# A transformer layer on one core: where 26 gate rows are loaded, where a bias correction is turned, and when eight sub-norms run

## The chip, the cores and the metric

The kernel runs on one core of a Trainium2 chip. Its time is the device time of one execution in microseconds (us); the kernel before took 2425.93 us, the median of three runs (2421.64 to 2428.02). A core has five engines with an instruction queue each, and each works through its queue in order: PE (matrix products; PEld is its loading of the stationary operand), DVE (vector), ACT (scalar and copies), POOL, and SP, which here only issues DMA transfers. POOL issues transfers too, in a queue of its own.

## The reference, cut to what matters

One layer of a diffusion transformer over 512 latent tokens and 256 context tokens, width 2048, everything in float32. Six modulation vectors come from a product of a conditioning vector with a 2048 x 12288 matrix; context tokens have their own conditioning.

```python
mod_x = (silu(c) @ w_ada + b_ada)                  # 6 x 2048, cut into sh1, s1, g1, sh2, s2, g2
h  = rmsnorm(x, norm1_w) * (1 + s1) + sh1          # the same for the context with c_ctx
p  = h @ w_in                                      # q, k, v of 8 differential heads; latent q, latent kv, a shared rotary key
o_da  = rmsnorm(softmax(q1 k1') v - lam * softmax(q2 k2') v, subln_w) * 0.8      # 8 heads
o_mla = softmax(([q_nope, q_rope] . [k_nope, k_rope]) / sqrt(192)) v             # 8 latent heads
x  = x + g1 * (concat(o_da, o_mla) @ w_o)
h2 = rmsnorm(x, norm2_w) * (1 + s2) + sh2
x  = x + g2 * ((silu(conv3(h2 @ w_up_gate)) * (h2 @ w_up_u)) @ w_down)
out = rmsnorm(x, final_w)
```

## The kernel before, in words

Tokens lie along the free dimension, features on the 128 partitions. Every float32 product is made of three products of a coarser type: an operand is split into a high part (a cast on ACT) and a rest (a subtraction on DVE), and `mm3` (L107, L108, L109) multiplies high by high, high by rest and rest by high. A block of weights is 128 x 1024; it is loaded by SP into one of the `wr` buffers, cast to `wh` on ACT and its rest `wl` taken on DVE. The third product of a block needs its rest.

Each of the 96 rows of 128 modulation values is a product that DVE makes alone: `gemv` loads a 1 MB piece of the matrix into one of two `ada` buffers and multiplies it with the conditioning vector in one instruction (L174). 64 of these rows are made late, one at a time between other work (`next_gemv`): those of s2 first, then of g1, sh2 and g2. A row's load into a buffer waits for the product that read the buffer last.

The input projection is a list of steps whose order is written out by hand on all engines (a "manual schedule"). Step i runs a block on PE, casts block i+2 on ACT, runs its first task, takes the rest of block i+2 on DVE and issues the load of block i+4 on SP, and then runs its other tasks (`step`). The first 16 row blocks were multiplied before their shift was known, so for the first features a correction is made: `bias_products` puts the products of the shifts into two PSUM banks, `bias_rows` copies them to SBUF, `bias_turn` turns them into columns with six small products (L729), and `bias_out` copies the columns to `beta` (L733). The two banks are the ones that the next feature block needs. Steps 2 to 9 make the values of the first four heads (`value_block(0, ...)`, 12 pairs of column half and token tile each), step 10 is the first half of feature 1, step 11 its second half, and so on; `feature_keys` rotates a feature and writes it out as keys; `lay(t)` splits and writes a tile of values.

Behind the projection the order within each engine comes from a scheduler that looks at the code's order, the engines and the buffers. The differential heads write their outputs to memory. The latent heads come in pairs: `latent_pair` projects queries, keys and values of a pair, and is called while the pair before is running; each head makes its scores (which read the shared rotary keys `krh` and `krlz`, loaded once, L1014 and L1017), its softmax, one `sub_norm` of a differential head (L1023 to L1028: a load, a square on ACT, one product on PE, a root on ACT and DVE, six DVE instructions in all), and `weighted_values`, which transposes the weights into a bank `pt`, or with its last argument set into two more banks `f` besides.

The output projection has four groups of eight blocks (`w_o[g, kb]`). Each block has 24 products on PE. At the end of a group four tiles of `x` are loaded into three buffers `xr`, DVE adds the scaled result (L1116) and POOL writes it out. Before most blocks stands a gate row of `next_gemv`, loaded by POOL. At the head of this stage the code of before reads

```python
            if g or kb > 2:
                next_gemv(wo, 1, gp)
            wh, wl = wblock(w_o[g, kb])
```

Then come the gated MLP (two thirds of the time) and the final norm, in a manual schedule again.

Of the kernel before, what the change touches and what calls it, by code (L numbers as in the profile page):

```python
# [9 lines left out]
F32 = mybir.dt.float32  # L10
# [42 lines left out]
def layer_kernel(ctx: ExitStack, tc: tile.TileContext, small, rope, c_row, cc_row, x_t, ctx_t, ada, ada_k,  # L53
# [484 lines left out]
    def gemvs(count):  # L538
        return lambda: next_gemv(sp_, count, gp)
# [127 lines left out]
                if 1 in g and co is not None:  # L667
                    mm3(co, w, hc[kt], kt == 0, kt == KT - 1)

    def value_block(half, vo, n_, last):  # L670
        wh, wl = hl_w.pop(len(steps))
        order = [(j, t) for t in last for j in range(2)] if n_ == 7 else [(j, t) for j in range(2) for t in range(NKEY)]
        for j, t in order:
            kt = KB[half][n_] * 2 + j
            w = (wh[:, j * 512:(j + 1) * 512], wl[:, j * 512:(j + 1) * 512])
            src, o = (hx[kt], t * P) if t < 4 else (hc[kt], (t - 4) * P)
            mm3(vo[t], (src[0][:, o:o + P], src[1][:, o:o + P]), w, n_ == 0 and j == 0, n_ == 7 and j == 1)

    def step(block, *tasks):
        i = len(steps)  # L680
        block()
        cast(i + 2)
        for k, task in enumerate(tasks or [lambda: None]):
            task()
            if k == 0:
                low(i + 2)
                load(i + 4)
        steps.append(i)
# [37 lines left out]
    def bias_turn():  # L726
        for row, a in zip(raws["b"][1:], ac):
            for i in range(row.shape[1] // P):
                pe.matmul(a[:, 2 * i:2 * i + 2], row[:, i * P:(i + 1) * P], sel, start=True, stop=True)  # L729
# [5 lines left out]
    with tc.manual_schedule(engines=every):  # L735
        raws[4] = keep(lat0[4], None, raw_query())
        for f in (2, 3, 0, 1):
# [13 lines left out]
                [lambda: add_shift([2, 3, 4])],  # L751
                [lambda: add_shift([5, 6], gemvs(1))],
                [lambda: add_shift([7], gemvs(1)), gemvs(1)],
                [gemvs(1), gemvs(1)], [gemvs(1), gemvs(1)])
        for n_ in range(8):
            step(lambda: value_block(0, v0, n_, first), *plan[n_])
            if 2 < n_ < 7:
                bias_products(n_ - 3)
        bias_turn()

        def lay(t, own=False):
            return lambda: put_value(0, v0, t, [rtmp(F32R), rtmp(F32R)] if own else None)
# [8 lines left out]
        def latent(i, hf):  # L771
            if hf == 0:
                fs["q", i] = b_tile(), None
            half_feature(fs["q", i], hf)
# [4 lines left out]
        def block(f, hf, *more):  # L779
            def emit():  # L780
                feature(f, hf)
                for m in more:
                    m()
            return emit
# [1 line left out]
        def ckv_squares():  # L786
            squares("ckv", [with_bias(i) for i in range(2)], [raw_tile("nq") for _ in range(2)])

        step(block(1, 0), bias_out, lay(0), lay(5), gemvs(1), lay(1, True), gemvs(1))
        step(block(1, 1), lay(2), lay(3), gemvs(1), lay(4, True))  # L790
        step(block(2, 0), gemvs(1), feature_keys(1))
        step(block(2, 1), lambda: kept_keys(k_d[0], 2, gemvs(1)))
        step(block(3, 0), feature_keys(2, gemvs(1)))
# [10 lines left out]
        def keep_cq(i):  # L804
            cqs.append(keep(*fs["q", i])[:, :T])

        step(lambda: latent(0, 0), gemvs(1))
        step(lambda: latent(0, 1), feature_keys(6))
        step(lambda: latent(1, 0), gemvs(1), lambda: keep_cq(0))
        step(lambda: latent(1, 1), gemvs(1))  # L810
        step(lambda: latent(2, 0), gemvs(1), lambda: keep_cq(1))
        step(lambda: latent(2, 1), gemvs(1))

# [74 lines left out]
    def weighted_values(pool, ws, v, dst, last=False):  # L888
        po = b_tile("po", 1)
        for kt in range(NKEY):  # L890
            pt = b_tile("f", 2) if last and kt % 3 else b_tile("pt", 1)
            for qt in range(NQT):
                pe.transpose(pt[:, qt * P:(qt + 1) * P], ws[qt][:, kt * P:(kt + 1) * P], ident)  # L893
            wth, wtl = split_tiles(pool, ("wth", "wtl"), [P, T], 2, pt)
            mm3(po, v(kt), (wth, wtl), kt == 0, kt == NKEY - 1)
        sc.copy(dst, po)
# [113 lines left out]

    oraw = [None] * 16
    mb = tc.alloc_tile_pool(name="mb", bufs=1, side="right", reuse_waits="tile")
    krh, krlz = mb.tile([P, TT], F32R, name="krh"), mb.tile([P, 2, TT], F32R, name="krlz")
    nc.sync.dma_start(krh.bitcast(F32), kr_d[0])  # L1014
    for i, (r, z) in enumerate(((lo, hi), (hi, lo))):
# [3 lines left out]
    def sub_norm(h):  # L1019

        q, rs, t2 = (mb.tile([P, T], F32, tag=g, name=nm(g), bufs=1) for g in ("sq", "sr", "s2"))
        oraw[h] = b2k()
        nc.sync.dma_start(oraw[h], o_d[h])  # L1023
        sc.square(q, oraw[h])
        po = b_tile("f", 2)
        pe.matmul(po, ones32, q, start=True, stop=True)
        rstd(rs, po, P, mb.tile([P, T], F32, tag="sq", name=nm("s1"), bufs=1), t2)
        ve.scalar_tensor_tensor(out=oraw[h], in0=oraw[h], scalar=subs, in1=rs, op0=ALU.mult, op1=ALU.mult)  # L1028

    for h in range(NH):  # L1030
        i = h % 2
        if i == 0:
            qs, qn, kn, vs = nxt
        ws = []
        for qt in range(NQT):
            c = slice(qt * P, (qt + 1) * P)
            l = sm.tile([P, 1], F32, tag="ml", name=nm("ml"), bufs=4)
            p = scores_softmax([(qn[i][0][:, c], kn[i][0]), (qn[i][0][:, c], kn[i][1]), (qn[i][1][:, c], kn[i][0]),
                                (qs[i][:, c], krh), (qs[i][:, c], krlz[:, i])], mb, "w", 8, l)
            ve.reciprocal(l, l)  # L1040
            ve.tensor_scalar(out=p, in0=p, scalar1=l, scalar2=None, op0=ALU.mult)
            ws.append(p)
        if i == 0 and h + 2 < NH:
            nxt = latent_pair(h // 2 + 1)
        sub_norm(h)
        oraw[8 + h] = b2k()
        weighted_values(mb, ws, lambda kt: [v[:, i * P:(i + 1) * P] for v in vs[kt]], oraw[8 + h], h == NH - 1)
    mb.release()
    ma.release()
    mc.release()  # L1050
# [46 lines left out]
    for g in range(4):  # L1097
        if g % 2:
            outs = [b_tile() for _ in range(4)]
        else:  # L1100
            s0, s1 = s_tile(), s_tile()
            outs = [s0[:, :512], s0[:, 512:], s1[:, :512], s1[:, 512:]]
        for kb in range(8):
            if g or kb > 2:
                next_gemv(wo, 1, gp)
            wh, wl = wblock(w_o[g, kb])
            order = [(j, i) for j in range(2) for i in range(4)]
            for j, i in sorted(order, key=lambda t: t[1]) if kb == 7 else order:
                kt, o = kb * 2 + j, j * 512 + i * P
                mm3(outs[i], (wh[:, o:o + P], wl[:, o:o + P]), osp[kt], kt == 0, kt == 15)  # L1110
        for i in range(4):
            dt = g * 4 + i
            xr = wo.tile([P, T], F32, tag="xr", name=nm("xr"), bufs=3)
            nc.sync.dma_start(xr, x_t[dt])
            x = b2k()
            ve.scalar_tensor_tensor(out=x, in0=outs[i], scalar=modx[:, 32 + dt:33 + dt], in1=xr,  # L1116
                                    op0=ALU.mult, op1=ALU.add)
            x1.append(x)
            gp.dma_start(x1_d[dt], x)
            if g < 3:  # L1120
                add_square(wo, ss, x, dt == 0)
# [553 lines left out]
```

## Time and profile before

| | before |
|---|---|
| median of three runs | 2425.93 us (2421.64, 2425.93, 2428.02) |
| the profiled execution | 2423.42 us, its span 2421.6 us |
| PE busy | 2342.4 us, 97% of the span |
| DVE busy | 1774.9 us, 73% |
| ACT busy | 1099.8 us, 45% |
| POOL busy | 281.7 us, 12% |
| mean granted clock of PE | 0.991 |
| moved by DMA | 407.45 MB, mean 168 GB/s |

The span runs from the first to the last instruction. The page's 40 slices show PE at 8 or 9 tenths nearly everywhere, and the DMA engines at 5 to 9 tenths in the first seven slices and in slices 15 and 16 (the output projection), where 334 and 213 GB/s are moved. A wait in the profile is the idle time of an engine before an instruction, with the instruction or transfer that ended it.

### The profile page before, as it was taken

The numbers are of one execution on the slowest core, as the hardware profiler recorded it, in microseconds if no ns is written. First come the engines' busy times: TensorE is split into PE (matmuls) and PEld (weight loads), VectorE is DVE, ScalarE is ACT, GpSimd is POOL, SyncE is SP. The second block draws the span as 40 slices with busy tenths as digits, with TensorE's granted clock in tenths as the row PEclk, the third lists the DMA queues.
The fourth block names the chain that finished last, engine by engine and source line by source line (L and its number), as shares of the span: only waits on it lengthen the run. The fifth ranks groups of instructions, "written<-read, shape, count | busy, mean of one in ns | idle before, by whom it ended". The sixth has DMA issues, their size and how long they took to land.

```text
span 2421.6 us, 32339 instructions
## 1 busy us (share of the span) xinstructions
PE 2342.4 (97%) x12444; PEld 1969.0 (81%) x12444; DVE 1774.9 (73%) x2303; ACT 1099.8 (45%) x1660; POOL 281.7 (12%) x350
## 2 busy tenths in 40 slices
PE   8999999999899998999999999999999999999997
PEld 5787888777677787788888888888888888888887
DVE  5996786698787877597576767676767676676667
ACT  5322322455555621254454545454445454454543
POOL 0001000121100022200101010101011111111113
PEclk9999999999999999999999999999999999999999
DMA  9767776853301289613555454545555555555572
GB/s 381 276 225 282 289 283 257 231 151 106 127 33 48 72 324 334 213 58 130 140 134 145 129 147 124 152 120 156 122 157 122 157 122 150 129 140 138 135 213 79
DMA packets 141514, 407.45 MB, mean 168 GB/s; under 512 B 14880, under 2 KB 31792, under 8 KB 130736
## 3 DMA queue, kind: packets, MB, share of 16 engines
q1 hardware_dynamic: 103552, 271.15, 34.1%
q0 software_dynamic: 36656, 133.19, 21.2%
q8 instruction: 97, 1.59, 0.3%
q10 hardware_dynamic: 1152, 1.05, 0.1%
q14 instruction: 57, 0.47, 0.1%
HBM read 335.86 MB, written 69.48 MB: 167 GB/s over the span
## 4 chain that ended last, share of the span: by engine, by line
PE 77%; DVE 9%; issue 7%; DMA 4%; ACT 3%; POOL 2%; SPq 0%; DVEq 0%; POOLq 0%; ACTq 0%
PE y L1373 13%; PE b L107 9%; PE b L108 9%; PE b L109 9%; PE z L1373 6%; PE y L1375 6%; PE z L1375 3%; PE s L881 3%; PE x L1373 2%; PE s L108 2%; PE s L107 2%; PE s L109 2%; DMA ada<-in_ada 1%; PE x L1375 1%; PE pt L893 1%
## 5 line engine op out<-in xcount | busy, mean ns | idle before, releaser
L1394 POOL DMA_DIRECT2D x_d<-xs x160 | 140.4, 1020 | 1165.4 <-ACT xs L1393 1135.7
L107 PE MATMUL b<-ah,wh 128*128 128x512 f32 (+1 forms) x672 | 259.3, 386 | 0.0
L108 PE MATMUL b<-al,wh 128*128 128x512 f32 (+1 forms) x672 | 259.2, 386 | 0.0
L109 PE MATMUL b<-ah,wl 128*128 128x512 f32 (+1 forms) x672 | 258.3, 384 | 0.0
L1349 DVE TENSOR_TENSOR wl<-wr,wh 128x1024 fp32r<-128x1024 f32 x126 | 153.9, 1221 | 128.9 <-ACT wh L1343 128.9
L1349 DVE TENSOR_TENSOR wl<-rb,wh 128x1024 fp32r<-128x1024 f32 x124 | 151.3, 1221 | 127.8 <-ACT wh L1343 127.8
L1343 ACT CAST wh<-wr 128x1024 fp32r<-128x1024 f32 x126 | 132.2, 1049 | 206.4 <-PE b L108 100.7
L1343 ACT CAST wh<-rb 128x1024 fp32r<-128x1024 f32 x124 | 130.2, 1051 | 189.8 <-PE b L108 115.8
L1349 DVE TENSOR_TENSOR wl<-ws,wh 128x1024 fp32r<-128x1024 f32 x123 | 150.1, 1221 | 88.7 <-ACT wh L1343 88.7
L1343 ACT CAST wh<-ws 128x1024 fp32r<-128x1024 f32 x123 | 128.3, 1043 | 137.9 <-PE b L108 45.2
L174 DVE CUSTOM_DVE_ANT_0 ada<-ada,cb,smt 128x2048 f32<-128x2048 f32 x64 | 153.3, 2397 | 50.3 <-DMA ada<-in_ada 50.2
L109 PEld LDWEIGHTS b<-ah,wl 128*128 128x128 f32 x672 | 126.4, 188 | 25.5
L107 PE MATMUL b<-a2k,wh 128*128 128x512 f32 (+1 forms) x352 | 135.7, 388 | 11.0 <-DVE beta L733 5.9
L107 PEld LDWEIGHTS b<-ah,wh 128*128 128x128 f32 x672 | 126.7, 188 | 22.9
L108 PEld LDWEIGHTS b<-al,wh 128*128 128x128 f32 x672 | 126.7, 189 | 21.9
L109 PE MATMUL b<-a2k,wl 128*128 128x512 f32 (+1 forms) x352 | 134.0, 381 | 6.3 <-DVE wl L81 6.3
L80 ACT CAST wh<-wr 128x1024 fp32r<-128x1024 f32 (+2 forms) x64 | 64.0, 1002 | 120.1 <-PE s L108 37.1
L210 ACT CAST wh<-wr 128x1024 fp32r<-128x1024 f32 x38 | 39.9, 1051 | 150.4 <-PE b L109 41.9
L1373 PE MATMUL y<-b2k,wh 128*128 128x512 f32 x410 | 106.9, 391 | 0.0
L883 DVE TENSOR_REDUCE m<-s 128x1 f32<-128x768 f32 x96 | 90.4, 950 | 22.6 <-PE s L881 22.2
L1393 ACT ACTIVATE xs<-b,modx 128x512 f32<-128x512 f32 x160 | 100.8, 680 | 0.3 <-DMA x_d<-xs 0.3
L81 DVE TENSOR_TENSOR wl<-wr,wh 128x1024 fp32r<-128x1024 f32 (+2 forms) x64 | 76.4, 1196 | 30.5 <-ACT wh L80 30.4
(536 smaller groups left out, 6113.7 us busy)
## 6 DMA issues: line engine op xcount, KB each, us to landing
ada<-in_ada POOLq DMA_DIRECT2D x80, 1024.0 KB, 5.9
rb<-in_w_up SPq DMA_DIRECT2D x123, 512.0 KB, 4.4
wr<-in_w_dn SPq DMA_DIRECT2D x84, 512.0 KB, 4.0
x_d<-xs POOLq DMA_DIRECT2D x160, 256.0 KB, 6.0
wr<-in_w_up SPq DMA_DIRECT2D x53, 512.0 KB, 4.3
wr<-in_w_f SPq DMA_DIRECT2D x34, 512.0 KB, 6.1
adak<-in_ada_k SPq DMA_DIRECT2D x64, 256.0 KB, 5.4
wr<-in_w_o SPq DMA_DIRECT2D x32, 512.0 KB, 5.4
```

Source lines behind the costliest of these rows:

```text
L81: ve.tensor_tensor(dst_l, src, dst_h.bitcast(F32), op=ALU.subtract)
L107: pe.matmul(out, st[0], mv[0], start=start, stop=False, **kw)
L108: pe.matmul(out, st[0], mv[1], start=False, stop=False, **kw)
L109: pe.matmul(out, st[1], mv[0], start=False, stop=stop, **kw)
L174: ve.tensor_tensor_reduce(out=junk, in0=w, in1=vec, op0=ALU.mult, op1=ALU.add, scale=1.0, scalar=col("b_ada", j), accum_out=dst[:, j:j + 1])
L883: ve.tensor_reduce(out=m, in_=s[:, :TT], axis=AX.X, op=ALU.max, negate=True)
L1343: sc.copy(hi, raw)
L1349: ve.tensor_tensor(lo, raw, hi.bitcast(F32), op=ALU.subtract)
L1373: pe.matmul(o, w[j][0], hs[j], start=start and j == 0, stop=False, skip_group_check=True)
L1375: pe.matmul(o[:, h0], w[j][1], hs[j][:, h0], start=False, stop=j == 7, skip_group_check=True)
L1393: sc.mul(x, po, modx[:, 80 + dt:81 + dt])
L1394: gp.dma_start(x1_d[dt], x, accum_op=ALU.add)
```

## The change

Five edits are made together.

- `bias_turn` runs inside the last value block, after 6 of its 12 pairs, and `bias_out` in that step between its two gate rows; before, `bias_turn` ran behind the block, and `bias_out` as the first task of the next step.
- Three gate rows more are made in the projection (one in the second half of feature 1, two in the latent queries: 38 instead of 35 in all), and 26 instead of 29 in the output projection, where the last block of groups 1 to 3 has none.
- These 26 are loaded by SP, in the queue of the weights, instead of POOL.
- In the latent heads' memory the eight softmax tiles `w` are placed first, which moves `krh` and `krlz` by 24 KB per partition. Before, they lay where the differential heads keep their values; now they lie over those heads' rotation and weight tiles.
- The sub-norms run in three heads (2 in head 0, 3 in head 2, 3 in head 4) instead of one in each, and the last two heads instead of the last one use the further banks for their transposes.

```diff
-    def value_block(half, vo, n_, last):
+    def value_block(half, vo, n_, last, midway=None):
...
-        for j, t in order:
+        for k, (j, t) in enumerate(order):
+            if midway and k == len(order) // 2:
+                midway()
...
-                [gemvs(1), gemvs(1)], [gemvs(1), gemvs(1)])
+                [gemvs(1), gemvs(1)], [gemvs(1), bias_out, gemvs(1)])
         for n_ in range(8):
-            step(lambda: value_block(0, v0, n_, first), *plan[n_])
+            step(lambda: value_block(0, v0, n_, first, bias_turn if n_ == 7 else None), *plan[n_])
...
-        bias_turn()
...
-        step(block(1, 0), bias_out, lay(0), lay(5), gemvs(1), lay(1, True), gemvs(1))
-        step(block(1, 1), lay(2), lay(3), gemvs(1), lay(4, True))
+        step(block(1, 0), lay(0), lay(5), gemvs(1), lay(1, True), gemvs(1))
+        step(block(1, 1), lay(2), lay(3), gemvs(1), lay(4, True), gemvs(1))
...
-        step(lambda: latent(0, 0), gemvs(1))
+        step(lambda: latent(0, 0), gemvs(1), gemvs(1))
...
-        step(lambda: latent(1, 1), gemvs(1))
+        step(lambda: latent(1, 1), gemvs(1), gemvs(1))
...
     mb = tc.alloc_tile_pool(name="mb", bufs=1, side="right", reuse_waits="tile")
+    mb.tile([P, TT], F32, tag="w", name=nm("w"), bufs=8)
     krh, krlz = mb.tile([P, TT], F32R, name="krh"), mb.tile([P, 2, TT], F32R, name="krlz")
...
-        sub_norm(h)
+        for k in {0: (0, 1), 2: (2, 3, 4), 4: (5, 6, 7)}.get(h, ()):
+            sub_norm(k)
         oraw[8 + h] = b2k()
-        weighted_values(mb, ws, lambda kt: [v[:, i * P:(i + 1) * P] for v in vs[kt]], oraw[8 + h], h == NH - 1)
+        weighted_values(mb, ws, lambda kt: [v[:, i * P:(i + 1) * P] for v in vs[kt]], oraw[8 + h], h >= NH - 2)
...
-            if g or kb > 2:
-                next_gemv(wo, 1, gp)
+            if kb != 7 if g else kb > 2:
+                next_gemv(wo, 1)
```

DVE at the end of the first values (step 9 and the start of step 10). An ISA row with `ada` is a gate row, `wl` the rest of a weight block, `kl` the rest of a value tile that is laid away. Before:

```order
L174 ISA ada_2013,modx<-ada_2013,cb,smt 128x2048
L174 ISA modx 128x1
L213 TENSOR_TENSOR wl_2011<-wr_1906,wh_2010 128x1024
L1123 SCALAR_TENSOR_TENSOR a_93<-modx,smt 128x1
L174 ISA ada_2019,modx<-ada_2019,cb,smt 128x2048
L174 ISA modx 128x1
L733 COPY beta<-b_1432 128x8
L733 COPY beta<-b_1433 128x4
L213 TENSOR_TENSOR wl_2079<-wr_1959,wh_2078 128x1024
L81 TENSOR_TENSOR kl_2087<-b_1562,kh_2086 128x512
```

Now:

```order
L174 ISA ada_2019,modx<-ada_2019,cb,smt 128x2048
L174 ISA modx 128x1
L213 TENSOR_TENSOR wl_2017<-wr_1906,wh_2016 128x1024
L735 COPY beta<-b_1432 128x8
L735 COPY beta<-b_1433 128x4
L174 ISA ada_2027,modx<-ada_2027,cb,smt 128x2048
L174 ISA modx 128x1
L81 TENSOR_TENSOR kl_2084<-b_1562,kh_2083 128x512
L213 TENSOR_TENSOR wl_2081<-wr_1959,wh_2080 128x1024
```

The two copies to `beta` stand one gate row earlier, and the first value tile is split before the next weight block's rest instead of behind it.

DVE in steps 11 and 12, where one gate row is added (`kl` of s and `rt` of s are the value tiles of step 11, L152 begins the rotation of feature 1). Before:

```order
L81 TENSOR_TENSOR kl_2171<-s_1561,kh_2170 128x512
L174 ISA ada_2176,modx<-ada_2176,cb,smt 128x2048
L174 ISA modx 128x1
L81 TENSOR_TENSOR rt_2180<-s_1561,rt_2179 128x512
L174 ISA ada_2238,modx<-ada_2238,cb,smt 128x2048
L174 ISA modx 128x1
L1123 SCALAR_TENSOR_TENSOR a_93<-modx,smt 128x1 x2
L213 TENSOR_TENSOR wl_2236<-wr_2084,wh_2235 128x1024
L152 TENSOR_TENSOR rt_2244<-b_2028,ropet 128x512
```

Now:

```order
L81 TENSOR_TENSOR kl_2171<-s_1561,kh_2170 128x512
L174 ISA ada_2176,modx<-ada_2176,cb,smt 128x2048
L174 ISA modx 128x1
L81 TENSOR_TENSOR rt_2180<-s_1561,rt_2179 128x512
L1126 SCALAR_TENSOR_TENSOR a_93<-modx,smt 128x1
L174 ISA ada_2185,modx<-ada_2185,cb,smt 128x2048
L174 ISA modx 128x1
L1126 SCALAR_TENSOR_TENSOR a_93<-modx,smt 128x1 x5
L174 ISA ada_2241,modx<-ada_2241,cb,smt 128x2048
L174 ISA modx 128x1
L213 TENSOR_TENSOR wl_2239<-wr_2090,wh_2238 128x1024
L152 TENSOR_TENSOR rt_2247<-b_2030,ropet 128x512
```

Three gate rows instead of two stand before the rest of block 14 (the last `wl`) and the rotation behind it.

SP in the output projection, in group 1 up to the first block of group 2 (the first `xr` is the last `x` tile of group 0). Before, weights and `x` tiles alone:

```order
L1114 DMA xr_7954<-in_x_t 128x512
L1114 DMA xr_8230<-in_x_t 128x512
L89 DMA wr_8101<-in_w_o 128x1024
L1114 DMA xr_8238<-in_x_t 128x512
L1114 DMA xr_8246<-in_x_t 128x512
L89 DMA wr_8134<-in_w_o 128x1024
L89 DMA wr_8167<-in_w_o 128x1024
L89 DMA wr_8200<-in_w_o 128x1024
L89 DMA wr_8267<-in_w_o 128x1024
```

Now, from the same place on:

```order
L171 DMA ada_8174<-in_ada 128x2048
L89 DMA wr_8177<-in_w_o 128x1024
L89 DMA wr_8207<-in_w_o 128x1024
L1117 DMA xr_8237<-in_x_t 128x512
L1117 DMA xr_8245<-in_x_t 128x512
L1117 DMA xr_8253<-in_x_t 128x512
L171 DMA ada_8271<-in_ada 128x2048
L89 DMA wr_8274<-in_w_o 128x1024
L171 DMA ada_8304<-in_ada 128x2048
L89 DMA wr_8307<-in_w_o 128x1024
```

Gate rows and weight blocks now alternate in one queue, the gate row ahead of the block of the same number. At the load of `krh` the order on SP is the same as before: right behind the load of the rotary query weights of the last pair (`w_uqr`).

## The prediction

> **What bounds the kernel now.** I read the shares of busy time first, then the waits of PE, then the windows around its longest waits.
>
> ```profile
> PE 2342.4 (97%) x12444; PEld 1969.0 (81%) x12444; DVE 1774.9 (73%) x2303; ACT 1099.8 (45%) x1660; POOL 281.7 (12%) x350
> PE b L109 <- DVE wl L81: 6.3, 2, 5.1
> PE b L107 <- DVE beta L733: 5.9, 1, 5.9
> PE s L109 <- DVE wl L81: 5.8, 2, 4.5
> PE s L881 <- DMA krh<-kr_d: 2.2, 1, 2.2
> ```
>
> PE is the bound: nothing in the diff takes products away, so the change can only remove idle time of PE and time at a low clock. The four waits (us in total, times, longest) are those in the places of the diff: 20.2 us together. Around three of them the clock falls too. A row of a window gives its length, then busy time and count of PE, PEld, DVE, ACT and POOL, PE's granted clock, the DMA engines' share and GB/s:
>
> ```profile
> 225.96:236.20 10.24, 5.21 (x15) 4.42 (x16) 8.41 (x12) 0.95 (x2) 1.15 (x3) 0.50 0.89 321
> 942.77:946.17 3.40, 3.40 (x9) 2.67 (x8) 3.40 (x3) 0.86 (x1) 0.94 (x2) 0.50 0.95 364
> 987.14:990.54 3.40, 3.13 (x7) 2.48 (x8) 3.40 (x2) 0.74 (x1) 3.38 (x3) 0.50 0.90 312
> 843.00:1031.00 188.00, 175.31 (x747) 141.75 (x746) 126.09 (x118) 47.13 (x58) 42.44 (x55) 0.98 0.79 291
> ```
>
> The first three are at half clock: work of 5.21, 3.40 and 3.13 us would take half of that, so 2.6, 1.7 and 1.6 us more go with the waits. The fourth is the output projection: DVE is idle for a third of it.
>
> **The correction (place A).** Rows of the timeline give start, length, engine, instruction, and in brackets the idle time before it and what ended it.
>
> ```profile
> 223.10 2.35 DVE L174 CUSTOM_DVE_ANT_0 ada<-ada,cb,smt 128x2048 f32<-128x2048 f32 x1 [0.73 <-DMA ada<-in_ada]
> 223.69 1.39 PE L729 MATMUL b<-sel,bias 128*128 128x2 f32 x12
> 225.38 1.22 DVE L213 TENSOR_TENSOR wl<-wr,wh 128x1024 fp32r<-128x1024 f32 x1
> 228.50 2.35 DVE L174 CUSTOM_DVE_ANT_0 ada<-ada,cb,smt 128x2048 f32<-128x2048 f32 x1 [1.83 <-DMA ada<-in_ada]
> 230.77 0.23 DVE L733 COPY beta<-b 128x8 f32<-128x8 f32 x2
> 230.99 0.80 PE L107 MATMUL b<-a2k,wh 128*128 128x512 f32 x1 [5.90 <-DVE beta L733]
> ```
>
> PE turns the correction by 225.09, then waits until DVE has copied it, and that copy stands behind a gate row whose load lands late. Now it stands right behind the rest at 225.38: 225.38 + 1.22 + 0.23 = 226.8. PE's wait becomes 226.8 − 225.1 = 1.7 instead of 5.9: 4.1 us less. A wait that short should leave the clock up: 2.6 more. A gives 6.7 at its place.
>
> A gate row is then late two steps on. Step 11 now has a third row ahead of the rest of block 14 and the rotation. Here the views are the timeline, and of the tile `ada` the times from issue to landing, over the whole run and then between 240 and 262 us; the last row is the window of that stretch.
>
> ```profile
> 249.89 0.53 POOL L171 DMA_DIRECT2D ada<-in_ada  x1 [9.64 <-DVE modx L174]
> 250.12 2.34 DVE L174 CUSTOM_DVE_ANT_0 ada<-ada,cb,smt 128x2048 f32<-128x2048 f32 x1
> 253.75 0.68 DVE L152 TENSOR_TENSOR rt<-b,ropet 128x512 f32<-128x512 f32 x1
> 257.24 0.01 DVE L153 LOAD_MASK_SELECT rt<-b  x1 [2.80 <-DMA v_d<-rt]
> 267.63 1.22 DVE L213 TENSOR_TENSOR wl<-wr,wh 128x1024 fp32r<-128x1024 f32 x1
> 275.52 1.05 ACT L210 CAST wh<-wr 128x1024 fp32r<-128x1024 f32 x1 [3.29 <-PE s L108]
> DMA to landing us min/median/max: 4.8/5.9/10.6
> DMA to landing us min/median/max: 7.1/7.6/8.4
> 236.20:260.00 23.80, 23.80 (x138) 20.84 (x137) 14.66 (x23) 4.56 (x8) 1.81 (x4) 1.00 0.98 370
> ```
>
> The buffer of the third row comes free when the first row of the step has read it, so its load goes out at 249.9. It lands at 254.7 at best and 260.5 at worst; the DMA engines are full here (share 0.98), so I take the local 7.6: 257.5. Behind it DVE has the row (2.35), the rest of block 14 (1.22), L152 (0.68) and then the shuffle, which before could start at 257.24 only, behind its own transfer: 4.1 us after the landing, 261.6. From the shuffle to the end of the rest of block 15, DVE took 268.85 − 257.24 = 11.6, and that chain has few gaps, so this rest now ends at landing + 15.7: 270.4, 273.2 or 276.2. Step 15 needs it: PE let go of ACT there at 275.5, which becomes 268.8 with A's 6.7, and the third product, which reads the rest, comes about 0.5 later. So PE waits 1.2 at best, 4.0 by the local landing, 7.0 at worst. I take 4.0: A is worth 6.7 − 4.0 = 2.7 net, with bounds of 5.5 and, with a half-clock stretch of 1.7 behind the longest wait, −2.0. The two rows added among the latent queries lie in steps where PE sets the pace and DVE waits for ACT's cast, and ACT for PE, so that a row of 2.35 fits; I cost them at nothing (uncovered: 4.7).
>
> **The keys' memory (place B).**
>
> ```profile
> 659.08 0.53 DVE L81 TENSOR_TENSOR wl<-wr,wh 128x384 fp32r<-128x384 f32 x1
> 659.64 0.33 SPq L89 DMA_DIRECT2D wr<-in_w_uqr  x1
> 660.02 0.42 SPq L1014 DMA_DIRECT2D krh<-kr_d  x1
> 663.41 0.73 PE L881 MATMUL s<-krh,qs 128*128 128x512 f32 x2 [2.22 <-DMA krh<-kr_d]
> ```
>
> The load of `krh` leaves SP right behind the load of the rotary query weights, which leaves when DVE frees its buffer (659.08 + 0.53 = 659.61). The order on SP stays, so a free destination does not let it leave sooner. I take 0; the other bound is the whole wait, 2.2.
>
> **The gate rows of the output projection (place C).** The rows are DVE's and PE's timeline, then the issues in this stage (count, KB each, median us to landing), and last the landings of all `wr` there.
>
> ```profile
> 940.27 0.75 DVE L1116 SCALAR_TENSOR_TENSOR b2k<-b,modx,xr 128x512 f32<-128x512 f32 x1 [5.42 <-DMA xr<-in_x_t]
> 942.21 0.50 PE L109 MATMUL s<-a2k,wl 128*128 128x512 f32 x1 [4.49 <-DVE wl L81]
> 982.54 2.35 DVE L174 CUSTOM_DVE_ANT_0 ada<-ada,cb,smt 128x2048 f32<-128x2048 f32 x1 [4.80 <-DMA ada<-in_ada]
> 987.41 0.79 PE L109 MATMUL b<-a2k,wl 128*128 128x512 f32 x1 [5.11 <-DVE wl L81]
> ada<-in_ada POOLq DMA_DIRECT2D x28, 1024.0 KB, 6.3
> wr<-in_w_o SPq DMA_DIRECT2D x25, 512.0 KB, 5.9
> DMA to landing us min/median/max: 3.4/5.4/11.0
> ```
>
> PE's waits for `wl` are not for DVE's work, which is one row (2.35) and one rest (1.22) against 175.31/32 = 5.5 us of PE per block. DVE sits idle for a load, of an `x` tile at 940 and of a gate row at 982, and the finished weights behind it wait. What can go is 6.3 + 5.8 = 12.1 of waits and 1.7 + 1.6 of clock: 15.4. For it speaks that no row is left in the last block of a group, where four `x` tiles and four results share the engines, that 3 MB less are moved (about 10 us of transfer at 291 GB/s), and that `wl` of the next group now stands ahead of the last of the four results. Against it: a row now shares SP's queue, and its issue waits until DVE has read the buffer, with the weights of the same block behind it. From that reading, the pair must land and be cast (1.05, as at 275.52) within two blocks, 11.0, so within 9.9; a row takes 6.3 now, so there is room. Of the four waits I leave one small one with one half-clock stretch, 3.4, and take 12. The lower bound is the slower rival's.
>
> [...]
>
> **The sub-norms (place D).** Two windows, the heads up to the last pair and the last ones, and a group of DVE's instructions in them:
>
> ```profile
> 666.00:792.00 126.00, 122.12 (x687) 99.69 (x686) 99.52 (x178) 72.27 (x142) 0.00 (x0) 1.00 0.12 39
> 792.00:846.00 54.00, 50.16 (x252) 37.55 (x251) 45.11 (x75) 32.06 (x62) 0.77 (x2) 1.00 0.20 70
> L1028 DVE SCALAR_TENSOR_TENSOR b2k<-b2k,subs,sr 128x512 f32<-128x512 f32 x8 | 6.0, 745 | 0.0
> ```
>
> PE idles 3.9 and 3.8 us there. A norm is six DVE instructions; at this row's 0.7 that is some 4.1 us. Out of the last heads go norms 6 and 7, in a window where DVE is busy for 84%, so at best its 3.8 are won. Three norms in one head bring 8.2 more than before, while DVE's idle time is (126.0 − 99.5 + 54.0 − 45.1)/8 = 4.4 per head, so at worst heads 2 and 4 lose 3.8 each, 7.6. Nothing on PE needs a norm's result before the output projection, so the work can slide; I take a gain of 1.
>
> **The sum.** 2.7 + 0 + 12 + 1 = 15.7. The profiled execution took 2423.4, which is 2.5 below the median of the runs; 2423.4 − 15.7 + 2.5 = **2410**. Its own range is 2404 to 2416.
>
> **Rivals.**
> *Everything is had:* A at 5.5, all of C, the last heads' 3.8 and the keys' 2.2 give 26.9: 2399. For it: each wait has a single cause. Against it: the full engines at 240 to 260, and SP's order at the keys.
> *Late weights:* the pair of row and weights lands in the 11.0 that the slowest `wr` took. Two blocks then take 11.0 + 1.05 = 12.05 instead of 11.0; over 26 rows, 13 pairs, 13.7 us come back, C is worth 1.7, the sum 5.4: 2420. For it: the engines' share of 0.79 leaves little. Against it: fewer bytes, spread more evenly.
> *Slower, the queue in series:* a pair takes the two medians one behind the other, 6.3 + 5.9 = 12.2. Two blocks take 13.25, PE waits 2.25 × 13 = 29 where it waited 15.4, so C costs 14 and A and D leave 10: 2436. It is slower than before from a landing of 11.4 on (15.4 + 3.7 over 13, plus 9.9). Against it: two buffers and weights issued ahead of need at first.
> *Step 15 pays:* the third row lands at its worst, A costs 2.0 and C and D hold: 11.0 gained, 2415.
>
> **How the numbers follow.** Forecast 0.52, everything 0.14, late weights 0.16, step 15 0.09, slower 0.09. A measurement here can tell about 0.3% from no change, 7.3 us: faster is below 2418.6, which the forecast, the first and the fourth case are, less a tail: 0.74; no change 0.18, mostly late weights; slower 0.08. The range is 2399 to 2423: it leaves out the series case and the ends of the two cases beside the forecast, some 0.2.
>
> **What would show it.** PE's wait for `beta` at about 1.7, and no half clock at 226 to 236. A wait of PE around 265 to 271 for `wl`, behind a gate row of step 11 that landed after 255. The load of `krh` still right behind that of `w_uqr`, and PE's 2.2 before L881 unchanged. In the output projection PE's waits for `wl` near 3 in sum, and rows and weights in SP's queue landing within 9.9 us of issue; if DVE's waits for `wr`'s casts grow instead, weights are late and the third or fourth case holds. PE's idle time in the last heads below 3.8. The forecast is wrong if a row in one queue lands far from 6.3 us, or if a third row in step 11 lands early enough to cost nothing.

## The result, and the profile after

The changed kernel takes 2408.43 us, the median of four runs (2403.19 to 2408.74); the kernel before, with a fourth run, 2423.78. The ratio is 0.9932, with a 95% interval of 0.9908 to 0.9956: some 16 us faster. The forecast was 2410. The profiled execution has a span of 2406.6 us, 15.0 less than before.

The first view is the busy time and then the waits of PE after the change (us in total, times, longest):

```profile
PE 2337.9 (97%) x12444; PEld 1967.4 (82%) x12444; DVE 1774.7 (74%) x2303; ACT 1100.5 (46%) x1660; POOL 271.2 (11%) x324
...
PE b L109 <- DVE wl L213: 3.3, 1, 3.3
PE s L882 <- DVE kl L81: 2.2, 1, 2.2
PE s L882 <- DMA krh<-kr_d: 1.9, 1, 1.9
PE b L107 <- DVE beta L735: 1.5, 1, 1.5
```

The wait for `beta` is 1.5 instead of 5.9, that for `krh` is nearly what it was, the two rows for `wl` of the output projection are gone, and a wait for `wl` of the projection is new (L213, 3.3). The 2.2 for `kl`, 1.5 before, stands before the first differential scores. To see where the time went I cut both spans at the same products of PE: the bias products of the first value step, the first differential scores, the first use of `krh`, and the sum of squares in the output projection. A row gives the length of the stretch, then busy time by engine, the clock, the DMA share and GB/s. Before:

```profile
185.86:439.01 253.15, 245.78 (x1228) 203.77 (x1227) 187.66 (x243) 70.56 (x104) 24.62 (x45) 0.98 0.76 277
439.01:663.41 224.40, 212.00 (x1045) 163.56 (x1045) 184.48 (x270) 124.30 (x234) 40.37 (x34) 1.00 0.51 150
663.41:1026.63 363.22, 343.08 (x1671) 276.81 (x1672) 266.38 (x363) 145.85 (x251) 42.05 (x55) 0.99 0.47 168
1026.63:2421.60 1394.97, 1369.42 (x7495) 1191.35 (x7493) 981.42 (x1207) 688.46 (x955) 162.19 (x188) 0.99 0.52 135
```

After:

```profile
186.72:439.17 252.45, 245.41 (x1228) 202.77 (x1227) 191.91 (x245) 68.57 (x102) 26.28 (x48) 0.99 0.80 290
439.17:663.55 224.38, 212.02 (x1045) 163.43 (x1045) 184.46 (x271) 124.37 (x234) 40.51 (x34) 1.00 0.51 152
663.55:1008.82 345.27, 337.30 (x1671) 275.16 (x1672) 260.41 (x357) 146.06 (x251) 29.39 (x26) 1.00 0.46 167
1008.82:2406.60 1397.78, 1370.40 (x7495) 1191.53 (x7493) 981.25 (x1207) 689.17 (x955) 162.47 (x188) 0.99 0.51 135
```

The third stretch, latent heads and output projection, gives 18.0, more than the whole. The first, with the correction and three of the extra steps, gives 0.7: PE is idle for 7.4 us in it before and for 7.0 after. The untouched parts, ahead of the first stretch (+0.9) and in the last (+2.8), moved the other way. In the same two stretches the twelve kernels below differ from each other by up to 3.4 and 3.7 us (5.5 in the last, with the changed kernel itself) although nothing in them was edited, so a difference of that size there is no effect of the change.

### The profile page after: what moved, and what is told of

Read it like the earlier page. It is cut to its first block, busy times and chain, and to the rows that moved or that the text cites. A ratio compares the mean times of both kernels' runs of the same rounds, so it can differ in the third digit from the quotient of the medians.

```text
span 2406.6 us, 32350 instructions
## 1 busy us (share of the span) xinstructions
PE 2337.9 (97%) x12444; PEld 1967.4 (82%) x12444; DVE 1774.7 (74%) x2303; ACT 1100.5 (46%) x1660; POOL 271.2 (11%) x324
## 4 chain that ended last, share of the span: by engine, by line
PE 69%; issue 14%; DVE 8%; ACT 3%; DMA 3%; POOL 2%; SPq 0%; POOLq 0%; DVEq 0%; ACTq 0%
PE y L1376 11%; PE b L107 7%; PE b L108 7%; PE b L109 7%; PE z L1376 6%; PE y L1378 5%; PE s L882 3%; PE z L1378 3%; PE x L1376 2%; PE s L108 2%; PE s L107 2%; PE s L109 2%; PE pt L894 1%; PE f L107 1%; PE x L1378 1%
## 5 line engine op out<-in xcount | busy, mean ns | idle before, releaser
L109 PE MATMUL b<-ah,wl 128*128 128x512 f32 (+1 forms) x672 | 258.0, 384 | 0.0
```

The lines of the kernel that those rows point to most:

```text
L109: pe.matmul(out, st[1], mv[0], start=False, stop=stop, **kw)
```

## Experiments: the queue of the gate rows

The two halves of the edit of the output projection are taken apart. In the first kernel the changed one gets POOL's queue back:

```diff
-                next_gemv(wo, 1)
+                next_gemv(wo, 1, gp)
```

In the second the kernel before gets SP's queue and nothing else:

```diff
-                next_gemv(wo, 1, gp)
+                next_gemv(wo, 1)
```

> The changed kernel with the 26 gate rows of the output projection loaded by POOL's queue as before the change; which blocks have a row stays as in the change. Theory: the waits for wl in the output projection came from gate rows in a group's last block, beside the four x tiles and results, and from POOL's queue in equal parts; by this one of the two longest waits comes back, 4 to 5 us with 1.7 of clock, so 6 us slower than the changed kernel. Rival 1, the place of the rows does it: PE does not wait for wl here either, same as the changed kernel within 1 us. Rival 2, the queue does it: all four waits come back, 12 to 15 us slower.

> The kernel before with one edit: its 29 gate rows of the output projection are loaded by SP's queue; the last blocks of the groups keep their rows and all else is as before. Theory (both halves matter): some 6 to 8 of the 15.4 us go, and a wait for wl at one group's end stays. Rival 1, the queue does it: 13 to 15 us less than before and no wait of PE for wl of over 1 us. Rival 2, the place of the rows does it: the waits stay at 10 us or more in sum, and the time with them.

With POOL's queue the ratio to before is 0.9980 (0.9963 to 0.9997), 12 us slower than the change. With SP's queue alone it is 0.9934 (0.9916 to 0.9953): the whole gain of the five edits, from one of them. Both expectations, that queue and place share the gain, missed. In the profiles PE waits 9.5 us in two waits for `wl` here with POOL's queue (the profiled run took 2413.99 us, the fastest of twelve with a median of 2423.15, so it shows less of the cost than most):

```profile
PE s L109 <- DVE wl L81: 9.5, 2, 7.9
...
934.82 0.80 PE L109 MATMUL s<-a2k,wl 128*128 128x512 f32 x1 [7.86 <-DVE wl L81]
```

With SP's queue alone no wait for `wl` in this stage reaches the list, though all 29 rows and those in the groups' last blocks are there. The stretch from the first use of `krh` to the sum of squares takes 347.90 us there, 15.3 less than before. So the queue does it, and the place and number of the rows do nothing that shows.

Why is told less surely. A gate row does not land sooner. The lines are issue to landing, least, median and longest, of `ada`, `wr` and `xr` in this stage, first of the kernel before, then of SP's queue alone:

```profile
DMA to landing us min/median/max: 4.9/6.3/8.6
DMA to landing us min/median/max: 3.4/5.4/11.0
DMA to landing us min/median/max: 2.8/5.1/10.3
```

```profile
DMA to landing us min/median/max: 4.7/7.2/11.9
DMA to landing us min/median/max: 3.4/8.0/12.7
DMA to landing us min/median/max: 3.7/7.5/8.7
```

Rows and weights are later by a median of 0.9 and 2.6 us, and only the slowest `x` tile is sooner: 8.7 us instead of 10.3 (11.0 in the kernel with POOL's queue, 7.9 in the changed one). DVE's waits for gate rows, before, and then those for rows and `x` tiles with SP's queue alone, up to 1013 us:

```profile
DVE ada L174 <- DMA ada<-in_ada: 28.8, 18, 4.8
```

```profile
DVE ada L174 <- DMA ada<-in_ada: 28.1, 25, 3.6
DVE b2k L1116 <- DMA xr<-in_x_t: 1.0, 2, 0.7
```

The sum for the rows is the same, but with SP's queue they are many and short, and the wait of 5.4 us for an `x` tile is gone. (Before, three waits for `x` tiles take 9.1 us; the last of them, 1.9 for the last tile of the stage, has a counterpart of 2.4 at 1014 us with SP's queue, just behind these lines.) A block gives DVE nearly 2 us of slack (5.5 us of PE less 2.35 for a row and 1.22 for a rest), so waits that are spread cost PE nothing, and one of 5 us does: before, PE waits behind the one for the `x` tile at 940.27 and behind one of 4.8 for a row at 982.54.

What makes the slowest `x` tile land sooner in one queue is not shown by these runs. One way to be late is POOL's own order, in which rows stand behind writes of results. It did not hold back the two rows whose waits were longest: the one read at 982.54 left POOL at 974.07, 0.3 us after its buffer came free, and in the kernel with POOL's queue the one read at 928.50, for which DVE waits 5.0, left at 919.94, as soon after. They took some 8.5 us to land. Why landings of up to 11.9 us in SP's queue make DVE wait no longer than 3.6 stays open.

## Experiments: the correction and the third row of step 11

The first kernel is the one before with the move of `bias_turn` and `bias_out` alone, as in the diff of the change. The second is the changed one with the third row moved.

```diff
-        step(block(1, 1), lay(2), lay(3), gemvs(1), lay(4, True), gemvs(1))
+        step(block(1, 1), lay(2), lay(3), gemvs(1), lay(4, True))
...
-        step(lambda: latent(2, 1), gemvs(1))
+        step(lambda: latent(2, 1), gemvs(1), gemvs(1))
```

> The kernel before with the correction's move alone (turned after 6 of the 12 pairs of the last value block, copied between its two gate rows); no row added, nothing else changed. My theory: PE's wait for beta falls from 5.9 to about 1.5 us and the half clock behind it (10.2 us, 2.6 lost) goes, and since step 11 keeps two gate rows, no wait for the rest of block 15 appears: about 6.5 us less than before, ratio 0.9973. Rival 1, the earlier steps only bring forward a wait that the full DMA engines then set anyway (a wait for wl near 270 us also here): 2 us less or nothing. Rival 2, the clock falls after a wait of 1.5 us too: 4 us less.

> The changed kernel with one gate row moved from the second half of feature 1 to the end of the latent queries; the number of rows in each stage as in the change. My theory: PE's wait of 3.3 us for the rest of block 15 at 270 us and the half clock of 3.4 us behind it (1.7 lost) come from that row's late load alone, so both go and the kernel is 5 us faster than the changed one: a ratio to before of about 0.991 instead of 0.993. The row costs nothing where it is now. Rival: the shift by the correction makes step 15 early, and the wait stays at 3 us or comes up again a step or two later: no gain. A third way: the row at the end of the latent queries makes PE wait there by 2 us or more.

The correction alone measured 0.9981 (0.9967 to 0.9996), some 5 us faster than before; the changed kernel without the third row 0.9918 (0.9898 to 0.9938), which its interval does not tell from the change. First the changed kernel's own rows at step 15:

```profile
257.99 2.35 DVE L174 CUSTOM_DVE_ANT_0 ada<-ada,cb,smt 128x2048 f32<-128x2048 f32 x1 [2.40 <-DMA ada<-in_ada]
262.01 0.01 DVE L153 LOAD_MASK_SELECT rt<-b  x1
272.41 1.22 DVE L213 TENSOR_TENSOR wl<-wr,wh 128x1024 fp32r<-128x1024 f32 x1
273.69 0.50 PE L109 MATMUL b<-a2k,wl 128*128 128x512 f32 x1 [3.30 <-DVE wl L213]
273.69:277.74 4.05, 4.05 (x14) 3.43 (x15) 4.01 (x8) 0.62 (x1) 0.00 (x0) 0.58 0.80 307
```

The row lands at 258.0, the shuffle starts 4.0 later, the rest of block 15 ends 15.6 after the landing, and PE waits 3.3 and then runs 3.4 us at half clock. Without the third row both go. But in the profiles neither kernel keeps what it wins: both now wait before the first differential scores. The first row is PE of the correction alone, the others PE, DVE and SP of the kernel without the third row, where the last row is SP's wait in total, times and longest.

```profile
441.09 0.76 PE L882 MATMUL s<-ks,qs 128*128 128x512 f32 x1 [5.06 <-DMA ks<-k_d]
```

```profile
436.56 0.77 PE L882 MATMUL s<-ks,qs 128*128 128x512 f32 x1 [5.76 <-DMA ks<-k_d]
426.56 2.35 DVE L174 CUSTOM_DVE_ANT_0 ada<-ada,cb,smt 128x2048 f32<-128x2048 f32 x1 [1.65 <-DMA ada<-in_ada]
428.94 0.68 SPq L851 DMA_DIRECT2D ks<-k_d  x1
SPq L851 <- DVE modx L174: 2.6, 1, 2.6
```

SP issues the load of these keys at 428.94, when DVE has read the last gate row of the projection (426.56 + 2.35 = 428.91): the keys' buffers lie where that row lay. In the changed kernel this is at 431.85, behind a row that ends at 431.81. In the kernel of the correction alone it is the queries' load, ahead of the keys on SP, that waits for the last row. Behind the two waits PE runs at half clock, which the changed kernel does not have there: the first product takes 0.76 and 0.77 us, against 0.48 in the changed kernel, and in the kernel without the third row this lasts some 3.5 us, up to the end of the product that starts at 439.7. For the kernel without the third row that is 3.6 us more of waiting than in the changed one (5.8 against 2.2) and 1.7 for the clock, 5.3 in all, as much as the 5.0 that step 15 had cost. The profile of the correction alone is of its slowest run (2430.52, the median of twelve is 2423.50), so it shows how a gain is lost, not how much: by the times 1 to 8 us are kept. So the end of the projection hangs on the chain of gate rows, each of which waits for the landing of its load, and a PE that comes earlier waits longer. Two kernels test that: both go back to the rows' numbers of before in the steps up to the latent queries, and the second besides moves two rows out of the second values.

```diff
-        step(block(1, 1), lay(2), lay(3), gemvs(1), lay(4, True), gemvs(1))
+        step(block(1, 1), lay(2), lay(3), gemvs(1), lay(4, True))
...
-        step(lambda: latent(0, 0), gemvs(1), gemvs(1))
+        step(lambda: latent(0, 0), gemvs(1))
...
-        step(lambda: latent(1, 1), gemvs(1), gemvs(1))
+        step(lambda: latent(1, 1), gemvs(1))
...
-            if kb != 7 if g else kb > 2:
+            if g or kb > 2:
```

In the second the last condition is `g or kb > 0`, and

```diff
-        step(values(5), gemvs(1), gemvs(1))
-        step(values(6), gemvs(1))
+        step(values(5), gemvs(1))
+        step(values(6))
```

> The changed kernel with the number of gate rows in each stage as before (35 in the projection, 29 in the output projection, those by SP's queue, with rows in the groups' last blocks). Theory: the wait at step 15 and its half clock go (5 us), but the keys of the first differential head leave only when the last gate row of the second values has been read, which the earlier rows' loads set, so PE waits there 4 to 6 us instead of 2.2 and wins 1 to 2 us in all; in the output projection no wait of over 1 us for wl, as with SP's queue alone. About 1 us faster than the changed kernel, ratio 0.9925. Rival 1, all 5 us of step 15 are won: 0.991. Rival 2, the rows in the last blocks cost 3 us or more in the output projection: slower than the changed kernel.

> The same as the other kernel of this call, with two gate rows of the second values (the one of the seventh step and one of two of the sixth) moved to the output projection, which makes 33 and 31. Theory: the last row is read about 8 us earlier, the loads of the keys leave 5 us or more earlier, and PE's wait before the first differential head falls from 4 to 6 us to about 1 us, then for DVE's rests of its queries or values; 31 rows by SP's queue still cost PE nothing. 4 to 6 us faster than the other, ratio about 0.990 to 0.991. Rival 1, the wait there is set by DVE's and ACT's work behind the last weights: it stays above 3 us. Rival 2, the output projection pays: waits for wl of 3 us or more in its first group.

They measured 0.9911 (0.9888 to 0.9934) and 0.9905 (0.9881 to 0.9928). The rows are the stretch from the bias products to the first differential scores, of the first kernel and of the second, with the second's last gate row and its load of the keys:

```profile
186.37:439.95 253.58, 245.09 (x1228) 202.91 (x1227) 185.82 (x241) 69.17 (x102) 24.61 (x45) 0.99 0.76 277
```

```profile
187.37:432.84 245.47, 243.43 (x1227) 201.81 (x1227) 178.09 (x231) 67.68 (x99) 23.55 (x43) 1.00 0.77 283
415.23 2.35 DVE L174 CUSTOM_DVE_ANT_0 ada<-ada,cb,smt 128x2048 f32<-128x2048 f32 x1 [1.30 <-DMA ada<-in_ada]
420.09 0.63 SPq L851 DMA_DIRECT2D ks<-k_d  x1
432.84 0.39 PE L882 MATMUL s<-ks,qs 128*128 128x512 f32 x1
```

With the rows' numbers of before PE waits 5.5 us for the keys and the stretch is as long as in the kernel before, though its correction waits only 2.9 us and nothing waits at step 15. With two rows fewer at the end the keys leave 11 us earlier, PE does not wait for them at all, and the stretch is 8.1 us shorter than the other's (in the other kernels so far it took 249.9 to 255.3). The 31 rows behind it cost 1.3 us of waits in the output projection. Of the 8.1 us only 2.5 reach the end of the profile, where PE among other things waits 3.8 instead of 2.1 us for `krh`, and by the times the two kernels are not told apart.

## Experiments: the shared keys

The first of three kernels is the changed one with the loads on POOL:

```diff
-    nc.sync.dma_start(krh.bitcast(F32), kr_d[0])
+    gp.dma_start(krh.bitcast(F32), kr_d[0])
...
-        nc.sync.dma_start(krlz[r, i].bitcast(F32), kr_d[1][r])
+        gp.dma_start(krlz[r, i].bitcast(F32), kr_d[1][r])
```

The second is the changed one with the keys where they lay before, and the third has both edits:

```diff
-    mb.tile([P, TT], F32, tag="w", name=nm("w"), bufs=8)
```

> The changed kernel with the loads of krh and krlz issued by POOL instead of SP. In the changed kernel PE starts on krh at 663.55 when the load lands, but DVE ends the queries qs at 663.45 (662.05 + 1.40) too. My theory: in the new memory the load can leave near 655 us and lands before 660; PE's wait stays at 1.8 us and is ended by DVE's qs instead of the load, and only the 0.7 us for krlz behind it goes. So less than 1 us. Rival 1, the memory's release was worth the wait: PE's 1.9 and 0.7 go, 2.6 us. Rival 2, POOL's queue holds the load back and PE waits longer than 3 us.

> The changed kernel without the line that puts the eight softmax tiles first, so that krh and krlz lie where the differential heads keep their values. My theory: SP issues krh 0.4 us behind the load of w_uqr as in the changed kernel, PE waits 1.9 to 2.2 us for it, nothing is lost there. The scheduler's order of the heads differs too, so the latent heads may move by up to 2 us either way. Rival: the load leaves SP a us or more later, since the values are read by PE until about 658, and PE waits 1 us or more longer.

> The changed kernel with krh and krlz loaded by POOL, but in the memory where they lay before (where the differential heads keep their values). In the new memory POOL issued krh 21 us ahead of PE's use. Theory: here the load waits until PE has read the last values, about 4 us before the use, and a load takes 3 to 3.5 us to land, so PE waits 0 to 1 us for krh and 0.7 for krlz; most of the 2.4 us comes from the queue and the memory is worth under 1.5 us. Rival 1, the memory is needed: PE's wait stays at 1.5 us or more. Rival 2, the load leaves as early as in the new memory and the place has no part in it at all.

Each was run once for its profile, with times of 2404.96, 2410.68 and 2400.81. In the changed kernel SP's queue shows the order that the prediction spoke of:

```profile
660.05 0.33 SPq L89 DMA_DIRECT2D wr<-in_w_uqr  x1
660.43 0.42 SPq L1016 DMA_DIRECT2D krh<-kr_d  x1
663.55 0.73 PE L882 MATMUL s<-krh,qs 128*128 128x512 f32 x2 [1.92 <-DMA krh<-kr_d]
```

In the old place it is the same: SP issues `krh` 0.42 us behind `w_uqr` and PE waits 2.25. With POOL's queue the load leaves 21 us before its use, in the new place and in the old one:

```profile
644.48 0.59 POOL L1016 DMA_DIRECT2D krh<-kr_d  x1
665.54 0.62 PE L882 MATMUL s<-krh,qs 128*128 128x512 f32 x2
```

```profile
639.50 0.59 POOL L1015 DMA_DIRECT2D krh<-kr_d  x1
657.19 0.73 POOL L1017 MEMSET krlz<- 64x768 f32 x1 [17.10 <-PE po L109]
```

PE waits neither for `krh` nor for `krlz` in either place. I had expected DVE's queries `qs` to keep PE waiting; but the product starts 0.6 us before the instructions that write them (665.54 and 666.12), so it reads others, and these are the next pair's. I had also expected that the values hold the old place until shortly before the use: only `krlz` waited for them, and it still came in time. So SP's order was the whole cause, about 2.6 us with `krlz`, and the memory had no part.

## Experiments: the sub-norms and the banks

Each kernel is the changed one with one of the two edits of the heads undone. The first:

```diff
-        for k in {0: (0, 1), 2: (2, 3, 4), 4: (5, 6, 7)}.get(h, ()):
-            sub_norm(k)
+        sub_norm(h)
```

The second:

```diff
-        weighted_values(mb, ws, lambda kt: [v[:, i * P:(i + 1) * P] for v in vs[kt]], oraw[8 + h], h >= NH - 2)
+        weighted_values(mb, ws, lambda kt: [v[:, i * P:(i + 1) * P] for v in vs[kt]], oraw[8 + h], h == NH - 1)
```

> The changed kernel with one sub-norm in each of the eight heads again; the further banks as in the change. My theory: the change of the heads (664 to 843 us, about 6 us of idle PE) is within 1 us: the three norms in one head are off PE's path, and the last heads' gain of 1 to 2 us is lost here. Rival 1: the norms are the whole gain of the heads, 3 us or more of idle PE come back. Rival 2: the clusters of norms cost time, and PE's idle time falls here by 1 us or more.

> The changed kernel with the further banks for the transposes in the last head only, as before. My theory: PE's idle time between 790 and 846 us rises by 0.5 to 1.5 us, for transposes that wait for the one bank. Rival: the same within 0.3 us, since the norms moved away from these heads do all of it.

Each was run once (2412.98 and 2406.71 us). The windows run some 179.5 us from the first use of `krh`: the kernel before, the changed one, a norm in each head, and the bank in the last head only.

```profile
663.41:843.00 179.59, 171.58 (x934) 136.59 (x935) 142.17 (x248) 101.82 (x198) 0.57 (x1) 1.00 0.13 43
```

```profile
663.55:843.00 179.45, 171.47 (x940) 137.82 (x941) 147.28 (x259) 107.46 (x208) 0.00 (x0) 1.00 0.14 49
```

```profile
668.40:848.00 179.60, 171.53 (x930) 136.94 (x931) 142.98 (x250) 103.09 (x200) 0.00 (x0) 0.99 0.14 47
```

```profile
660.73:840.00 179.27, 171.13 (x917) 137.49 (x918) 143.26 (x253) 103.73 (x202) 0.00 (x0) 0.97 0.12 38
```

PE is idle for 8.0, 8.0, 8.1 and 8.1 us. Neither edit changes that. The changed kernel is 6 products ahead of the one before, some 1.1 us at the mean of these windows, which one profile each does not tell from chance. The last window's clock of 0.97 stands for some 10 us at half clock, which explains its fewer products. Behind the equal sums waits were exchanged: those for transposed weights (`wth` and `wtl`) are 2.9 us before, 2.8 with a norm in each head, 0.7 with the bank in the last head only and none that reaches the list in the changed kernel, but with the norms bunched, as in these last two, PE waits 1.6 us for their squares.

## Experiment: what the runs point to

The kernel with two rows fewer in the second values, and the keys by POOL (both edits as above).

> The changed kernel with two gate rows of the second values moved to the output projection and one each taken back from step 11 and the latent queries' two steps (33 in the projection, 31 behind it), and krh and krlz loaded by POOL. Theory: the two gains stand at different places and add: PE's idle time from the correction to the first differential head stays near 2 us, and the wait for krh and krlz, 3.8 us in the kernel without the last edit, is gone: about 3 us less than that, near 2402 by the median, a ratio of 0.9895. Rival: one of the two turns into another wait further on (for ACT's weights w, or for krlz), and the time is that of the kernel without the last edit, 0.9905.

It measured 2400.75 against 2424.94 for the kernel before, run beside it, a ratio of 0.9898 (0.9873 to 0.9923): 24 us faster than before, where the change gives 16. The two intervals overlap slightly. In its profile, of 2398.6 us, PE waits neither for the differential keys nor for `krh`, as expected. Its waits for ACT's weights `w` are 1.0 us longer than in the kernel without the last edit (5.9 and 4.9), so the rival, that a new wait eats one of the two gains, holds in part at most; by the times, 0.9898 and 0.9905, the two kernels are not told apart.

## Why the prediction was right, and where its parts were not

The sum, 15.7, stands against 15.0 in the profile, so its total was right, and the largest term lay where it was put. That it fits so well is partly luck: the heads and the output projection gave 5 us more than forecast, the stretch of the correction 2 less, and the untouched parts took 3.7 by scatter.

- **C, the output projection (forecast 12, measured 18 with the heads in it).** All four waits, 12.1, and the 3.3 of both half-clock stretches went; the remaining 2.5 is in PE's busy time, and no run here shows where it comes from. With SP's queue alone the stretch gives 15.3, which is the 15.4 that was at stake. What was mis-sized is the 3.4 that I left over. The reasons that I gave for it were not those that count: the empty last blocks and the 3 MB moved elsewhere, which I listed in its favour, did nothing that shows, and the shared queue, which I listed against it, did all. The limit of 9.9 us for a pair's landing was wrong as well: weights in one queue took up to 12.7 us without a wait of PE for them, so both rivals with late weights were priced too high.
- **A, the correction (2.7).** The wait for `beta` came to 1.5 (forecast 1.7), the half clock behind it went, and the row of step 11 cost 3.3 of wait (forecast 4.0) by the chain that was written down, at 4.0 and 15.6 us behind its landing. (The forecast has 4.1 and 15.7; its own terms, 2.35 + 1.22 + 0.68, add up to 4.25.) Two things were missed. A half-clock stretch of 3.4 us followed that wait, 1.7 us; it was only in the lower bound. And the step that failed is that the prediction followed the shift to step 15 only and not to the end of the stage, where the keys' load waits for the last gate row. How much of A that took is not known well. The whole stretch came out 0.7 shorter in this pair of profiles; but the two profiles with the old projection, edits elsewhere aside, have 253.2 and 255.3 us, and the seven with the new one 249.9 to 254.4 with a mean of 252.2, some 2 us less, which does not tell 0.7 from the forecast's 2.7. PE's wait before the scores is 0 to 5.2 us in these seven.
- **The two rows in the latent queries (0).** Nothing there shows a cost; they were not tried alone, and they belong to the chain of rows on which the keys' load hangs.
- **B, the keys' memory (0).** Right, and for the stated reason.
- **D, the sub-norms (1).** No effect in sum can be shown. The norm was priced at 4.1 us; six instructions of the 0.745 shown would be 4.5, which changes neither the term nor its sign.

Of the two things named as showing the forecast wrong neither came: rows in one queue landed after a median of 6.6 us, and the third row of step 11 had its cost. The sign of late weights did come. DVE's waits for casts of weights grew from 22.0 to 32.8 us, and weights took up to 11.1 us to land, over the limit of 9.9; but PE had no wait from it, so the sign was badly chosen.

## What to carry to other kernels

When transfers that feed one consumer share the engines with transfers of another queue, look at the longest wait, not only at the sum: here DVE waited 28 us for gate rows with either queue, and PE lost 12 us where waits of 4.8 for a row and 5.4 for an `x` tile were among DVE's, and nothing where none was above 3.6. Follow a saved wait to the end of its stage and ask which buffer the next stage's first load needs, and who reads it last: here two gate rows fewer let the keys leave 11 us earlier, and a wait of 5.5 us was gone. When a load is late, look first at what stands ahead of it in its issuing queue, and only then at its memory: for `krh` and `krlz` the queue was worth some 2.6 us of PE's waits and the place nothing.

## What was not expected of the hardware

The clock. A wait of 1.9 us for `krh` was followed by no slow stretch in the changed kernel (a clock of 1.00 from 663.55 to 675), by some 3.4 us at half clock in the kernel with a norm in each head (its window above stands at 0.99), and by 10.2 in the kernel with the correction alone:

```profile
668.31:678.55 10.24, 9.03 (x28) 7.40 (x28) 4.44 (x7) 2.86 (x6) 0.00 (x0) 0.50 0.02 6
```

In the profiles before and after the change the stretches at half clock (the one at the end of a run aside) are 3.4, 6.8 and 10.2 us long. What sets where one begins is not shown by these runs, and here the length of the wait ahead of it does not tell. The forecast took it that a wait as short as the one left for `beta` leaves the clock up, and behind its 1.5 us it did (1.00 from 227.65 to 240). But before the change a wait of 1.58 us that ended at 48.18 was followed by 3.4 us at half clock, and one of 2.22 for `krh` by none. And the wait for `beta` was 1.5, 0.5, 1.5, 2.1, 4.9, 3.9 and 1.9 us in the changed kernel and the six that share its projection: one profile is not the size of such a term, and the two with a long wait there had none at step 15, where the others waited 2.6 to 3.5.
